# Opening transfers, output tiles, gating of w_out and the static scheduler of a hybrid decoder block

## Chip, cores and metric

The kernel runs on one core of one Trainium2 chip. The metric is the device time of one execution in microseconds (us), the median of the runs. Engines are named as in the profile: PE is TensorE, DVE VectorE, ACT ScalarE, POOL GpSimd, SP SyncE, which issues the transfers.

## The reference

One sequence of 512 tokens, width 1024, passes through a decoder block in float32. A conditioning vector `c` gives six modulation vectors (shift, scale and gate for each of two sub-layers). One projection `w_in` feeds two mixers: sparse attention with an index score and a top-k of 128 keys per query, and a gated linear recurrence. Their outputs are gated and added, go through `w_out`, and a convolutional FFN follows. Cut to that:

```python
c_act = jax.nn.silu(c)
mod = jnp.dot(c_act, w_ada[l]) + b_ada[l]
sh1, sc1, ga1, sh2, sc2, ga2 = [m[:, None, :] for m in jnp.split(mod, 6, axis=-1)]
xn = rms_norm(h, g_mix[l]) * (1.0 + sc1) + sh1
proj = jnp.dot(xn, w_in[l]) + b_in[l]
q, k, v, qi, ki, wi, xr, yr, gate_a, gate_b = jnp.split(proj, cuts, axis=-1)
attn = dsa_attention(q, k, v, qi, ki, wi, rel_bias)      # q_idx, k_idx score; top_k; softmax
xr = causal_dwconv(xr, conv_rnn_w[l], conv_rnn_b[l])
rnn = rg_lru(xr, ...) * jax.nn.gelu(yr)                  # h = scan of a*h + u
merged = (jax.nn.sigmoid(gate_a) * jnp.dot(attn, w_o_attn[l])
          + jax.nn.sigmoid(gate_b) * jnp.dot(rnn, w_o_rnn[l]))
h = h + ga1 * jnp.dot(merged, w_out[l])
xn = rms_norm(h, g_ffn[l]) * (1.0 + sc2) + sh2
up = causal_dwconv(jnp.dot(xn, w_up[l]), conv_ffn_w[l], conv_ffn_b[l])
val, gte = jnp.split(up, 2, axis=-1)
h = h + ga2 * jnp.dot(jax.nn.silu(gte) * val, w_down[l])
return rms_norm(h, g_final)
```

## The kernel before

Every float32 product is three matmuls on TensorE: each operand is split into a rounded high part and a low rest (`xh`, `xl` of the activations, `wh`, `wl` of a weight), and `mm3` adds xh·wh, xl·wh and xh·wl. ScalarE writes the high part of a weight, VectorE subtracts it to get the low part. Weights come as 1 MB transfers of two output tiles each (`wr`; `wo` for w_out; `wa` for pieces of w_ada) into three landing buffers, and their parts lie in six buffers of 128x1024.

Every instruction is first recorded in a `Plan`. Then a list scheduler orders all of them by a rank and by what the cost of each would be, and the kernel is emitted in that order, a fixed order for each engine. An operation may name several engines (`("dve", "pool")`), of which the scheduler chooses one. The rank comes from `P.fix` (the planned time of a matmul) or from `P.soft`, a time that the code writes ahead of a group of operations. Numbers such as `COLD`, `SOON`, `RB`, `IW` and `AW` at the head of the file are such times and widths.

The stages, in TensorE's order:

- Opening. `x` is read in eight halves of 128x512, its row norms are computed, and its tiles `xs` are transposed. `dots` (VectorE) multiplies pieces of w_ada by `crow`, the silu of `c` spread over all partitions, and gives shift and scale (`modc`) for each block `kt` of 128 features. ScalarE makes `xf` from transposed `xs` and `modc`, then `xh`. A first group of seven tiles (`G0`) is multiplied block by block, its block 0 in two halves of 256 tokens.
- The rest of `w_in` in tiles of 128 output features, one `wr` half each: tiles 0 to 19 (`xr`, `yr`, `qi`, `k`, `v`, `q`), then the gates `gb` and `ga` (tiles 20 to 35).
- `rnn_batch` comes twice, each for four blocks: gates `rg` (two products, with `xc` and with `m`), the scan `h`, and `yr*h`. The products of `rg` and `yr` may go to VectorE or GpSimd.
- Index scores, top-k (MAX8 and MATCH_REPLACE8 in turn on VectorE), softmax, and attention run between the tiles.
- Output tiles `wr` (the recurrence) for j = 0 to 7, then `wa` (attention) for j = 0 to 7. `consume` multiplies each by its gate and, for `wa`, adds the two on VectorE or GpSimd and splits the sum into `mh`, `ml`.
- w_out: rows of the weight, `raw`, are multiplied by the gate vector `ga_b`, split into `woh`, `wol`, and used for four row tiles. The result is added to `x` (`xr_`).
- Second norm, FFN up and down projections, final norm.

## Time and profile before

| | |
|---|---|
| median of 3 runs | 808.45 us (807.95 to 808.86) |
| span of the profiled execution, first to last instruction | 807.4 us |
| device time of the profiled execution itself | not shown; its span is 1.05 us under the median |
| PE busy | 778.1 us, 96% |
| DVE busy | 605.1 us, 75% |
| ACT busy | 434.7 us, 54% |
| POOL busy | 83.3 us, 10% |
| bytes moved | 105.23 MB, 130 GB/s on average |

PE is busy in nearly all of the span. The other engines matter where PE waits for them; those waits are few and each can be found in a view of the waits.

### The profile page before, as it was taken

What the parts mean: (1) busy time and instruction counts of PE and PEld (TensorE: products, weight loads), DVE (VectorE), ACT (ScalarE), POOL (GpSimd) and SP (SyncE); (2) the same over time, 40 slices, a digit from 0 to 9 for tenths busy, and PEclk for the clock granted to TensorE, in tenths of its full rate; (3) what the DMA queues carried; (4) which work ended last, traced back from release to release, by engine and by line L of the source; (5) the groups of instructions that cost most, each with busy time, mean ns of one, the idle gap of its engine ahead of it and who ended that gap; (6) DMA issues with size and microseconds to landing.
All of it is one profiled execution on the core that took longest, in us unless ns stands there. A gap on an engine that the chain in (4) does not pass through costs nothing.

```text
span 807.4 us, 9805 instructions
## 1 busy us (share of the span) xinstructions
PE 778.1 (96%) x3576; PEld 646.3 (80%) x3576; DVE 605.1 (75%) x1137; ACT 434.7 (54%) x745; POOL 83.3 (10%) x88
## 2 busy tenths in 40 slices
PE   5999999999799999999899999999999999999996
PEld 3888778888688888888688988888888888888885
DVE  5997975999999989757988777766556688774024
ACT  5679825579499989632427744434444454332013
POOL 2000300034331242003201000000000000000000
PEclk9999989999899999999999999999999999999999
DMA  9973132331121251537174233343222224431002
GB/s 323 391 259 133 53 105 104 105 106 53 52 86 73 106 207 60 203 116 254 73 297 172 102 124 144 153 157 131 104 103 69 89 105 157 146 123 60 12 26 79
DMA packets 21297, 105.23 MB, mean 130 GB/s; under 512 B 2376, under 2 KB 4864, under 8 KB 10624
## 3 DMA queue, kind: packets, MB, share of 16 engines
q1 hardware_dynamic: 21248, 104.60, 36.0%
q8 instruction: 28, 0.46, 0.2%
q14 instruction: 21, 0.17, 0.1%
HBM read 102.47 MB, written 3.69 MB: 131 GB/s over the span
## 4 chain that ended last, share of the span: by engine, by line
PE 77%; DVE 13%; ACT 4%; DMA 3%; issue 2%; POOL 1%; SPq 0%; POOLq 0%; ACTq 0%; DVEq 0%
PE ps L499 76%; DVE h L817 2%; PE ps L511 2%; DVE wl L435 1%; DVE wol L435 1%; DVE wo L435 1%; DVE wa L584 1%; DMA wr<-in_w_up_dram 1%; DMA x<-in_x_dram 1%; DMA wa<-in_wada_dram 1%; DVE rg L435 1%; POOL rstd L570 1%; DVE sc L860 1%; DVE m L859 1%; ACT rg L428 1%
## 5 line engine op out<-in xcount | busy, mean ns | idle before, releaser
L499 PE MATMUL ps<-yl,wh 128*128 128x512 f32 (+1 forms) x376 | 141.8, 377 | 0.3 <-DVE yl L435 0.2
L499 PE MATMUL ps<-yh,wh 128*128 128x512 f32 (+1 forms) x376 | 141.5, 376 | 0.0
L499 PE MATMUL ps<-yh,wl 128*128 128x512 f32 (+1 forms) x376 | 141.3, 376 | 0.0
L435 DVE TENSOR_TENSOR wl<-wr,wh 128x1024 fp32r<-128x1024 f32 (+1 forms) x96 | 117.3, 1222 | 29.2 <-ACT wh L428 29.2
L428 ACT ACTIVATE wh<-wr 128x1024 fp32r<-128x1024 f32 (+1 forms) x96 | 97.8, 1019 | 63.8 <-PE ps L499 60.5
L499 PE MATMUL ps<-xh,wl 128*128 128x512 f32 x288 | 114.7, 398 | 7.9 <-DVE wl L435 7.9
L499 PE MATMUL ps<-xh,wh 128*128 128x512 f32 x288 | 114.8, 399 | 0.0
L499 PE MATMUL ps<-xl,wh 128*128 128x512 f32 x288 | 114.2, 396 | 0.0
L440 DVE SCALAR_TENSOR_TENSOR cv<-ps,ct,cv 128x511 f32<-128x511 f32 (+1 forms) x88 | 65.6, 747 | 42.5 <-ACT cv L428 41.1
L499 PEld LDWEIGHTS ps<-yl,wh 128*128 128x128 f32 x376 | 70.8, 188 | 13.7 <-DVE yl L435 1.0
L499 PEld LDWEIGHTS ps<-yh,wh 128*128 128x128 f32 x376 | 70.8, 188 | 12.9
L499 PEld LDWEIGHTS ps<-yh,wl 128*128 128x128 f32 x376 | 70.8, 188 | 12.7
L499 PEld LDWEIGHTS ps<-xh,wl 128*128 128x128 f32 x288 | 55.4, 192 | 20.6 <-DVE wl L435 8.7
L428 ACT ACTIVATE cv<-ps,ct 128x512 f32<-128x512 f32 x44 | 33.8, 768 | 67.8 <-PE ps L499 67.8
L499 PE MATMUL ps<-dl,acth 128*128 128x512 f32 (+1 forms) x181 | 69.4, 384 | 0.0
L499 PE MATMUL ps<-dh,actl 128*128 128x512 f32 (+1 forms) x181 | 69.4, 383 | 0.0
L499 PE MATMUL ps<-dh,acth 128*128 128x512 f32 (+1 forms) x181 | 69.4, 383 | 0.0
L499 PEld LDWEIGHTS ps<-xl,wh 128*128 128x128 f32 x288 | 55.3, 192 | 10.8
L499 PEld LDWEIGHTS ps<-xh,wh 128*128 128x128 f32 x288 | 55.4, 192 | 10.5
L584 DVE SCALAR_TENSOR_TENSOR wa<-wa,crow 128x1024 f32<-128x1024 f32 x48 | 59.6, 1257 | 2.7 <-DMA wa<-in_wada_dram 2.7
L570 POOL TENSOR_TENSOR rstd<-ms,mhalf 128x1 f32<-128x1 f32 x12 | 9.3, 783 | 415.1 <-DVE ms L440 415.1
L428 ACT ACTIVATE dh<-wd 128x512 fp32r<-128x512 f32 x44 | 25.9, 626 | 35.3 <-PE ps L499 31.5
(242 smaller groups left out, 1440.3 us busy)
## 6 DMA issues: line engine op xcount, KB each, us to landing
wa<-in_wada_dram SPq DMA_DIRECT2D x22, 1024.0 KB, 5.6
wr<-in_w_up_dram SPq DMA_DIRECT2D x22, 1024.0 KB, 4.8
wr<-in_win_dram SPq DMA_DIRECT2D x18, 1024.0 KB, 4.8
wd<-in_w_down_dram SPq DMA_DIRECT2D x11, 1024.0 KB, 4.8
wr<-in_wo_rnn_dram SPq DMA_DIRECT2D x4, 1024.0 KB, 4.8
wo<-in_w_out_dram SPq DMA_DIRECT2D x4, 1024.0 KB, 4.7
x<-in_x_dram SPq DMA_DIRECT2D x8, 256.0 KB, 4.7
wa<-in_wada_dram SPq DMA_DIRECT2D x4, 512.0 KB, 6.4
```

What stands on the lines that cost most here:

```text
L428: nc.scalar.activation(real(dst), real(src), func, **kw)
L435: lambda e: ENG[e].tensor_tensor(real(dst), real(a), real(b), op=op), tag="tt")
L440: lambda e: nc.vector.scalar_tensor_tensor(real(dst), real(a), real(s), real(b), op0=op0, op1=op1), tag="stt")
L499: nc.tensor.matmul(real(ps), real(a), real(b), start=st, stop=sp)
L511: nc.tensor.transpose(real(ps[:, i * 128:(i + 1) * 128]), real(s), real(ident))
L570: lambda: nc.gpsimd.tensor_tensor(real(r), real(ms), real(mhalf), op=ALU.pow), "pool")
L584: vop(1.14, [r, crow], [r, dst], lambda: nc.vector.scalar_tensor_tensor(real(r), real(r), 1.0, real(crow), op0=ALU.mult, op1=ALU.mult, acc ...
L817: vop(0.61, [a, u], [h], lambda h=h, a=a, u=u: nc.vector.tensor_tensor_scan(real(h), real(a), real(u), 0.0, op0=ALU.mult, op1=ALU.add))
L859: vop(0.07 + 0.00104 * W, [a], [m8], lambda m8=m8: nc.vector.max(real(m8), real(a)))
L860: vop(0.07 + 0.00104 * W, [a, m8], [a], lambda m8=m8: nc.vector.match_replace(real(a), real(m8), real(a), TAKEN))
```

## The change

These things change together.

1. Opening transfers: all of `x` for the first two row tiles comes right behind the small table `ct`, then both halves of the first `wa` block, then the rest of `x`, then weights. The relative bias table moves behind the third `wa`. Squares of row tiles 2 and 3 are on ScalarE alone. Eight calls of `transposes` on the identity, 32 instructions, write a bank that is otherwise empty then.
2. Output tiles: `OUTS` gives an order in which `wr` and `wa` tiles alternate in groups. The one of a pair that comes second makes the sum, on VectorE only.
3. The gate of w_out: `ga_b` no longer multiplies the weight; the result of each of the eight output pieces is multiplied by it instead.
4. Scheduler: operations that read two SBUF operands on VectorE or any on GpSimd are marked as sharing a port (`shares_port`), and one is not planned beside the other. The cost of a matmul, a scan, MAX and MATCH_REPLACE is other than before.
5. `INFLATE`, `HORIZON`, `SOON`, `LATER`, `CLOCK` and the step widths of the index and attention stages take other values.
6. Where the scheduler may choose, GpSimd gets one product of the RNN batches instead of twelve.
7. The order of each engine is changed by all of these. On ScalarE 29 table loads stand where 26 stood, one of the new ones ahead of the square roots of the first RNN batch.

```diff
+OUTS = [("wr", (0, 1, 2, 3)), ("wa", (0, 1)), ("wr", (4, 5)), ("wa", (2, 3, 4, 5, 6, 7)), ("wr", (6, 7))]
-COLD = 17.0
+COLD = 8.0
+WARM = 8
+DOT1 = 13.6
+def pass_us(n):
+    return max(0.109, 0.0133 + n / 2400)
...
+    def shares_port(engs, reads, writes, tag):
+
+        wide = [vw(v) for v in reads if isinstance(v, (Buf, View)) and vw(v).bx[1][1] - vw(v).bx[1][0] > 1]
+        sbuf = [v for v in wide if v.buf.kind != "b"]
+        out = set()
+        if "pool" in engs and (sbuf or tag == "pow"):
+            out.add("pool")
+        if "dve" in engs and (len(sbuf) > 1 or (sbuf and tag in ("ts", "sc", "sq", "dot"))):
+            out.add("dve")
+        return out
...
+                if e in o.shares:
+                    f = "pool" if e == "dve" else "dve"
+                    t = max(t, port[f])
+                    for p in avail[f]:
+                        begin = max(free[f], p.ready, p.after)
+                        if f in p.shares and p.rank < o.rank - 2 and not p.allocs and begin < t + 0.3:
+                            t = max(t, begin + p.engs[f])
...
-            P.soft = -59.0 + 2 * t + h + 5 * (t > 1)
+            P.soft = -70.0 + 2 * t + h if t < 2 else -56.0 + 2 * t + h
...
+    xs = [normed(xt[t], LATER, ("act", "dve") if t < 2 else ("act",)) for t in range(TT)]
...
+    for n in range(WARM):
+        P.soft, P.after = -43.0, 3.7
+        transposes(g0ps[-1], [ident] * 4)
+    P.soft, P.after = None, 0.0
...
-            vop(0.61, [a, u], [h], lambda h=h, a=a, u=u: nc.vector.tensor_tensor_scan(
+            vop(1.13, [a, u], [h], lambda h=h, a=a, u=u: nc.vector.tensor_tensor_scan(
...
-        elif kind == "wr":
-            s = got["gb", j]
+        elif kind in ("wr", "wa"):
+            s = got["gb" if kind == "wr" else "ga", j]
             tt(s, ps, s, ALU.mult)
-            mid.append(s)
-        elif kind == "wa":
-            s = got["ga", j]
-            tt(s, ps, s, ALU.mult)
-            tt(s, s, mid[j], ALU.add, ("dve", "pool"))
+            if j not in mid:
+                mid[j] = s
+                return
+            tt(s, s, mid[j], ALU.add)
             hi, lo = t2(F32R, name="mh"), t2(F32R, name="ml")
             split(hi, lo, s)
-            merged.append((hi, lo))
+            merged[j] = (hi, lo)
...
-                tt(r, r, ga_b[0][h], ALU.mult)
                 split(hi, lo, r)
...
-            tt(xr_, ps, xr_, ALU.add)
+            gated = t2(name="gated")
+            tt(gated, ps, ga_b[0][h], ALU.mult)
+            tt(xr_, gated, xr_, ALU.add)
```

How this moves instructions is seen at three places. The first is TensorE's start, before: `csil` matmuls spread the silu of `c`, `oh` is the relative bias, `xs` are row tiles of the normalised `x`, and `w0h` the high part of the first weight.

```order
L499 MATMUL ps_113<-ident_89,csil_98 128x128
L499 MATMUL ps_117<-ident_89,csil_98 128x128
L499 MATMUL ps_113<-ident_89,csil_98 128x128 x3
L499 MATMUL ps_117<-ident_89,csil_98 128x128 x3
L499 MATMUL ps_147<-oh_79,rb_85 128x384
L511 MATMUL ps_163<-ident_89,xs_132 128x128
L511 MATMUL ps_163<-ident_89,xs_155 128x128
L499 MATMUL ps_209<-xh_192,w0h_168 128x256
L499 MATMUL ps_209<-xl_193,w0h_168 128x256
```

The same place in the changed kernel, where `ps_210`, `ps_246` and `ps_251` receive the transposes of block 0.

```order
L530 MATMUL ps_120<-ident_79,csil_98 128x128 x3
L530 MATMUL ps_129<-ident_79,csil_98 128x128 x3
L542 MATMUL ps_110<-ident_79 128x128 x28
L542 MATMUL ps_210<-ident_79,xs_137 128x128
L542 MATMUL ps_210<-ident_79,xs_146 128x128
L542 MATMUL ps_246<-ident_79,xs_235 128x128
L542 MATMUL ps_246<-ident_79,xs_237 128x128
L542 MATMUL ps_251<-ident_79,xs_137 128x128
L542 MATMUL ps_251<-ident_79,xs_146 128x128
L542 MATMUL ps_251<-ident_79,xs_235 128x128
L542 MATMUL ps_251<-ident_79,xs_237 128x128
L530 MATMUL ps_261<-xh_232,w0h_227 128x256
```

Identity transposes now stand ahead of and behind the `csil` matmuls, the relative bias is gone from here, and the eight transposes of all row tiles stand ahead of the first matmul with `xh`, which was behind two of them.

The second place is VectorE in the first RNN batch, before; `wl_1007` is the low part that TensorE waits for at 102.90 us.

```order
L435 TENSOR_TENSOR rg_860<-rg_860,m_938 128x512
L435 TENSOR_TENSOR rg_880<-rg_880,m_953 128x512
L817 SCALAR_TENSOR_TENSOR h_1004<-a_916,rg_846 128x512
L817 SCALAR_TENSOR_TENSOR h_1009<-a_929,rg_860 128x512
L817 SCALAR_TENSOR_TENSOR h_1015<-a_936,rg_872 128x512
L817 SCALAR_TENSOR_TENSOR h_1022<-a_943,rg_880 128x512
L435 TENSOR_TENSOR yr_736<-yr_736,h_1015 128x512
L435 TENSOR_TENSOR yr_776<-yr_776,h_1022 128x512
L440 SCALAR_TENSOR_TENSOR qi_959<-ps_765,ct_81,qi_959 64x512
L440 SCALAR_TENSOR_TENSOR qi_993<-ps_765,ct_81,qi_993 64x512
L440 SCALAR_TENSOR_TENSOR xc_999<-ps_882,ct_81,xc_999 128x511
L435 TENSOR_TENSOR wl_1007<-wr_699,wh_1006 128x1024
```

The same place in the changed kernel, where that low part is `wl_1018`.

```order
L466 TENSOR_TENSOR rg_889<-rg_889,m_967 128x512
L466 TENSOR_TENSOR rg_900<-rg_900,m_975 128x512
L854 SCALAR_TENSOR_TENSOR h_1029<-a_938,rg_867 128x512
L854 SCALAR_TENSOR_TENSOR h_1039<-a_950,rg_877 128x512
L854 SCALAR_TENSOR_TENSOR h_1048<-a_957,rg_889 128x512
L854 SCALAR_TENSOR_TENSOR h_1062<-a_961,rg_900 128x512
L466 TENSOR_TENSOR yr_751<-yr_751,h_1029 128x512
L466 TENSOR_TENSOR yr_757<-yr_757,h_1039 128x512
L466 TENSOR_TENSOR yr_764<-yr_764,h_1048 128x512
L466 TENSOR_TENSOR yr_924<-yr_924,h_1062 128x512
L466 TENSOR_TENSOR wl_1018<-wr_719,wh_1017 128x1024
L471 SCALAR_TENSOR_TENSOR qi_1027<-ps_807,ct_84,qi_1027 64x512
```

All four products of `rg` (two of them above these rows) and all four of `yr` are in VectorE's order, where two and two stood, and the low part of the weight stands directly behind the last of them, ahead of `qi` and `xc`.

The third place is VectorE between the low parts of tiles 22 and 23, before (`sc` is the index score, `m` the eight largest, `q` the queries).

```order
L435 TENSOR_TENSOR wl_1901<-wr_1648,wh_1900 128x1024
L859 MAX m_360_1970<-sc_1531 128x8
L440 SCALAR_TENSOR_TENSOR q_1914<-ps_1773,ct_81,q_1914 64x512
L860 MATCH_REPLACE sc_1531<-m_360_1970,sc_1531 128x384
L440 SCALAR_TENSOR_TENSOR q_1920<-ps_1773,ct_81,q_1920 64x512
L859 MAX m_361_1988<-sc_1531 128x8
L440 SCALAR_TENSOR_TENSOR q_1928<-ps_1824,ct_81,q_1928 64x512
L860 MATCH_REPLACE sc_1531<-m_361_1988,sc_1531 128x384
L435 TENSOR_TENSOR wl_1938<-wr_1648,wh_1937 128x1024
```

In the changed kernel the low parts are `wl_1914` and `wl_1955`. Here stand the last twelve of the rows from the one to the other; behind `wl_1914` come twelve more of the same kinds.

```order
L896 MAX m_361_2063<-sc_1560 128x8
L938 ISA l_2072,nmax_2073<-ps_2041,bm_1990 128x128
L938 ISA nmax_2073 128x1
L897 MATCH_REPLACE sc_1560<-m_361_2063,sc_1560 128x384
L471 SCALAR_TENSOR_TENSOR q_1936<-ps_1804,ct_84,q_1936 64x512
L896 MAX m_362_2087<-sc_1560 128x8
L941 RECIPROCAL sums_2051<-sums_2051 128x1
L897 MATCH_REPLACE sc_1560<-m_362_2087,sc_1560 128x384
L941 RECIPROCAL sums_2070<-sums_2070 128x1
L941 RECIPROCAL sums_2076<-sums_2076 128x1
L941 RECIPROCAL sums_2081<-sums_2081 128x1
L466 TENSOR_TENSOR wl_1955<-wr_1555,wh_1954 128x1024
```

Seven instructions stood between the two; now there are 23, with softmax passes (`ISA`, with `nmax`) and reciprocals among them.

## Rows read from the trace of the kernel before

**Rows 1.** First part of the page: busy us, share of the span, instructions.
```profile
PE 778.1 (96%) x3576; PEld 646.3 (80%) x3576; DVE 605.1 (75%) x1137; ACT 434.7 (54%) x745; POOL 83.3 (10%) x88
```

**Rows 2.** Waits of TensorE: engine, line, waited for; us, times, longest.
```profile
PE ps L499 <- DVE wl L435: 7.9, 2, 4.5
...
PE ps L499 <- DVE wol L435: 2.3, 1, 2.3
```

**Rows 3.** Windows: us, busy of PE, PEld, DVE, ACT, POOL, clock, DMA share, GB/s.
```profile
200.00:220.00 20.00, 15.49 (x62) 12.41 (x61) 19.57 (x41) 7.93 (x17) 7.97 (x9) 0.83 0.15 53
209.00:214.00 5.00, 4.89 (x12) 3.83 (x13) 4.80 (x11) 0.00 (x0) 0.00 (x0) 0.50 0.00 0
```

**Rows 4.** Timeline of TensorE, 99 to 108: start, us, engine, line, instruction, idle before.
```profile
99.13 0.39 PE L499 MATMUL ps<-xl,wh 128*128 128x512 f32 x1
102.90 0.80 PE L499 MATMUL ps<-xh,wl 128*128 128x512 f32 x1 [3.38 <-DVE wl L435]
103.49 0.63 PE L499 MATMUL ps<-xh,wh 128*128 128x512 f32 x1
...
107.76 0.63 PE L499 MATMUL ps<-xl,wh 128*128 128x512 f32 x1
```

**Rows 5.** Timeline of TensorE in the opening.
```profile
15.95 0.58 PE L499 MATMUL ps<-xh,w0h 128*128 128x256 f32 x1 [2.33 <-ACT xh L428]
...
25.03 0.40 PE L499 MATMUL ps<-xh,w0h 128*128 128x512 f32 x1
25.26 0.40 PE L499 MATMUL ps<-xl,w0h 128*128 128x512 f32 x1
```

**Rows 6.** Timeline of VectorE in the first RNN batch; x counts instructions put together.
```profile
88.13 3.49 DVE L435 TENSOR_TENSOR rg<-rg,m 128x512 f32<-128x512 f32 x2
91.55 6.67 DVE L817 TENSOR_TENSOR_SCAN h<-a,rg 128x512 f32<-128x512 f32 x4
98.14 1.26 DVE L435 TENSOR_TENSOR yr<-yr,h 128x512 f32<-128x512 f32 x2
...
101.62 1.22 DVE L435 TENSOR_TENSOR wl<-wr,wh 128x1024 fp32r<-128x1024 f32 x1
```

**Rows 7.** Timeline of GpSimd in the same stretch.
```profile
92.84 4.30 POOL L435 TENSOR_TENSOR yr<-yr,h 128x512 f32<-128x512 f32 x2 [1.76 <-DVE h L817]
```

**Rows 8.** The tile of the scans: ns of one, shortest, median and longest.
```profile
L817 DVE TENSOR_TENSOR_SCAN h<-a,rg x8: 1191/1727/2252, 91.5 to 200.6; 128x512 f32<-128x512 f32 x8
```

**Rows 9.** Timeline of ScalarE in the first RNN batch.
```profile
85.49 1.28 ACT L428 ACT_TABLE_LOAD   x1
```

**Rows 10.** Timeline of VectorE in the second RNN batch.
```profile
174.92 2.10 DVE L435 TENSOR_TENSOR wl<-wr,wh 128x1024 fp32r<-128x1024 f32 x1
...
193.88 2.38 DVE L435 TENSOR_TENSOR rg<-rg,m 128x512 f32<-128x512 f32 x2
196.18 6.66 DVE L817 TENSOR_TENSOR_SCAN h<-a,rg 128x512 f32<-128x512 f32 x4
```

**Rows 11.** VectorE's instructions by line and shape: busy us, mean ns, idle before.
```profile
L435 DVE TENSOR_TENSOR wo<-wo,ga 128x512 f32<-128x512 f32 x16 | 11.6, 750 | 1.7 <-DMA wo<-in_w_out_dram 1.7
...
L859 DVE MAX8 m<-sc 128x8 f32<-128x384 f32 x16 | 8.9, 557 | 0.3
...
L901 DVE CUSTOM_DVE_ANT_0 l<-ps,bm 128x128 f32<-128x128 f32 x8 | 1.8, 281 | 0.0
```

**Rows 12.** GpSimd's instructions by line and shape.
```profile
L435 POOL TENSOR_TENSOR ga<-ga,gb 128x512 f32<-128x512 f32 x8 | 12.8, 1607 | 71.4 <-DVE ga L435 68.9 <-ACT woh L428 2.5
```

**Rows 13.** Last part of the page: transfers, KB each, median us to landing.
```profile
wo<-in_w_out_dram SPq DMA_DIRECT2D x4, 1024.0 KB, 4.7
```

**Rows 14.** Timeline of VectorE in the opening.
```profile
9.88 0.69 DVE L469 SCALAR_TENSOR_TENSOR junk<-x 128x512 f32<-128x512 f32 x1 [1.77 <-DMA x<-in_x_dram]
...
10.70 1.22 DVE L584 SCALAR_TENSOR_TENSOR wa<-wa,crow 128x1024 f32<-128x1024 f32 x1
```

**Rows 15.** Waits of ScalarE.
```profile
ACT wh L428 <- PE ps L499: 60.5, 37, 10.0
```

More of the change, by code (lines that the diff above doesn't have):

```diff
@@ L43 @@
 SHAPES = {"W": [128, 2048], "w": [128, 1024], "t": [128, 512], "b": [128, 512]}
-INFLATE = 1.3
-HORIZON = 32
+INFLATE = 1.19
+HORIZON = 26
 EARLY = 3
 LAST = 5
+OUTS = [("wr", (0, 1, 2, 3)), ("wa", (0, 1)), ("wr", (4, 5)), ("wa", (2, 3, 4, 5, 6, 7)), ("wr", (6, 7))]
 ADA0 = 28
-COLD = 17.0
-SECOND = 0.0
-LATER = 20.93
-CLOCK = 11.0
+COLD = 8.0
+RBIAS = [14.0, 46.0, 48.0]
+WARM = 8
+DOT1 = 13.6
+SECOND = -25.0
+LATER = 19.39
+CLOCK = 12.7
 RB = [3.28, 5.94, 7.96, 11.0, 13.85, 0.61]
-SOON = [17.32, 14.96, 25.0, 9.88]
-ISTEP = {1: 13, 2: 36, 3: 83}
-IW = {1: 18, 2: 46, 3: 37}
+SOON = [20.62, 17.45, 25.0, 11.19]
+ISTEP = {1: 13, 2: 37.5, 3: 88.8}
+IW = {1: 18, 2: 46.8, 3: 42.2}
 ASTEP = {0: 76, 1: 93, 2: 126, 3: 145}
-AW = [8, 16, 15, 29]
-BUMP = [0.2, 0.93]
+AW = [8, 13.5, 18.7, 30.4]
+BUMP = [0.16, 0.81]
 def tile_columns(kind, j):
@@ L154 @@
     __slots__ = ("engs", "emit", "reads", "writes", "deps", "succ", "rank", "idx", "func", "ready", "left",
-                 "fixed", "soft", "hor", "after", "weak", "allocs", "lat", "end", "bufs", "start", "eng", "n", "tag")
+                 "fixed", "soft", "hor", "after", "weak", "allocs", "lat", "end", "bufs", "start", "eng", "n", "tag", "shares")
 LAT = {"pe": {"pe": 0.0, "act": 0.2, "dve": 0.2, "pool": 0.2, "sp": 0.2},
@@ L178, in op @@
         o.n, o.tag = n, tag
+        o.shares = self.shares_port(engs, reads, writes, tag)
         o.soft, o.hor, o.after = self.soft, self.hor, self.after
@@ L244, in order @@
         avail = {e: [] for e in LAT}
+        port = {"dve": 0.0, "pool": 0.0}
         free = {e: 0.0 for e in LAT}
@@ L335, in order @@
             free[e] = o.end
+            if e in o.shares:
+                port[e] = o.end
             for x in o.engs:
@@ L482, in scaled, with vop @@
         P.op({e: c[e] for e in engs}, [src, s], [dst], emit, tag="sc")
-    def vop(cost, reads, writes, fn, eng="dve", n=1):
-        P.op({eng: cost}, reads, writes, lambda e: fn(), n=n, tag="vop")
+    def vop(cost, reads, writes, fn, eng="dve", n=1, tag="vop"):
+        P.op({eng: cost}, reads, writes, lambda e: fn(), n=n, tag=tag)
     def mm(group):
@@ L492, in mm @@
             fp = vw(b).buf.dtype == F32
-            cost += max(0.107, 0.00042 * n) if not fp else max(0.214, 0.00168 * n)
+            cost += 2 * pass_us(2 * n) if fp else pass_us(n)
             reads += [a, b]
@@ L529, in col @@
         return ct[:, o + j:o + j + n]
-    P.soft = -60.0
+    P.soft = -90.0
     dma(ct, cols, 128 * 4 * NCOLS)
@@ L562, in rstd_of @@
         for h, v in enumerate(halves):
-            square(t2(name="junk")[:, :width(v)], v, parts[h])
+            square(t2(name="junk")[:, :width(v)], v, parts[h], engs)
             if h == 0:
@@ L569, in rstd_of, with normed @@
         vop(0.46, [ms, mhalf], [r],
-            lambda: nc.gpsimd.tensor_tensor(real(r), real(ms), real(mhalf), op=ALU.pow), "pool")
+            lambda: nc.gpsimd.tensor_tensor(real(r), real(ms), real(mhalf), op=ALU.pow), "pool", tag="pow")
         return r
-    def normed(halves, after=0.0):
-        r = rstd_of(halves)
+    def normed(halves, after=0.0, engs=("act", "dve")):
+        r = rstd_of(halves, engs)
         o = [t2(name="xs") for _ in range(2)]
@@ L609, in modulate @@
         return hi, lo
-    xs = [normed(xt[t], LATER) for t in range(TT)]
+    xs = [normed(xt[t], LATER, ("act", "dve") if t < 2 else ("act",)) for t in range(TT)]
     rb, oh, bias = cst((128, 128), "rb"), t2(name="oh"), t2(name="bias")
@@ L614, in block_kernel @@
     vop(0.5, [], [oh], lambda: nc.gpsimd.memset(real(oh), 0.0), "pool")
-    P.soft = -54.5
+    P.soft = RBIAS[0]
     dma(rb[:32, :8], rel_bias, 1024)
     dma(oh[:32, :NU], onehot, 32 * 4 * NU)
-    P.soft = -10.0
+    P.soft = RBIAS[1]
     pb = bank()
     mm([(pb[:, :NU], rb, oh[:, :NU], True, True)])
-    P.soft = 16.0
+    P.soft = RBIAS[2]
     act(bias[:8, :NU], pb[:8, :NU], AF.Copy, scale=8.0)
@@ L630, in block_kernel @@
         if kt < 2:
-            P.soft = -55.0 + 15 * kt
+            P.soft = -60.0 + 20.0 * kt
             dma(raw[:, 1, :], wada1[kt, :, 1, :], 1 << 19)
-            P.soft = -54.0 + 15 * kt
+            P.soft = -58.0 + 20.0 * kt
             dma(raw[:, 0, :], wada1[kt, :, 0, :], 1 << 19)
-            P.soft = -52.0 + 15 * kt
+            P.soft = -45.0 + 8 * kt
         else:
@@ L644, in block_kernel @@
         sh, sc = small((128, 1), "sh"), small((128, 1), "sc")
+        P.after = DOT1 if kt else 0.0
         dots(sc, raw, 1)
@@ L648, in block_kernel @@
         tt(modc[:, kt:kt + 1], sh, col("b_ada", kt), ALU.add)
+        P.after = 0.0
         ws = []
@@ L708, in block_kernel @@
     order += [byname["gb", j] for j in range(8)] + [byname["ga", j] for j in range(8)]
-    order += [("wr", j, wo_rnn, j // 2, j % 2, KT) for j in range(8)]
-    order += [("wa", j, wo_attn, j // 2, j % 2, 4) for j in range(8)]
+    for kind, js in OUTS:
+        order += [(kind, j, wo_rnn, j // 2, j % 2, KT) if kind == "wr" else (kind, j, wo_attn, j // 2, j % 2, 4) for j in js]
     raws = {}
@@ L936, in block_kernel @@
     ga_b = [[None, None], [None, None]]
-    mid = []
-    merged = []
+    mid = {}
+    merged = {}
     def consume(kind, j, ps):
@@ L1162, in down @@
         hi, lo = dsplit[f][h]
-        planned(0.00127 * (n.stop - n.start))
+        planned(3 * pass_us(n.stop - n.start))
         mm3(ps[:, n], acts[f][0][:, c], acts[f][1][:, c], hi[:, n], lo[:, n], f == first, f == last)
```

17 lines of the change are left out of this document (9 added, 8 removed).

## The prediction

> **What bounds the kernel now.** The profiled execution has a span of 807.4 us; no device time is shown for that execution itself. The median of the three runs, 808.45 us, lies 1.05 above that span, so I make the sum on the span and add the 1.05 at the end. The page's first part has TensorE busy for 778.1 us of it [rows 1]: some 29 us of idleness, and what a low clock costs behind it, are all that the change can take. I read TensorE's waits next [rows 2]: two waits on the low half of a weight (`wl`) hold 7.9 us, the longer 4.5, and one on `wol` in the w_out stage 2.3. Then the windows [rows 3]: behind the longer one the granted clock is 0.50. The reader is to see that such a wait is paid twice. At the first one [rows 4] TensorE stands for 3.38 us until 102.90; from 103.49 to 107.76 ten matmuls take 4.27, 0.427 each, where in the opening two of the same width start 0.23 apart [rows 5]. About twelve and a half matmuls run at that pace, each 0.20 too slow: 2.5. So **stall 1** costs 5.9. **Stall 2** is the longer wait, 4.5, and the window from 209 to 214 holds 12 matmuls in 4.89 where 21 would fit: 2.2, together 6.7. **Stall 3** is 2.3 and, if it is paid at the rate of stall 1 (2.5 of clock on 3.4 of wait), 1.7 more: 4.0. The opening is the fourth place: from the first matmul of the projection (15.95) to the first of 512 columns (25.03) 9.08 us pass, in which stand 42 matmuls of 256 columns, worth 42 × 0.12 = 5.0 (half of 0.23 each), and some transposes.
>
> VectorE makes `wl`, so I ask what it did before stall 1 [rows 6]. Behind the previous `wl` stand two `rg*m` (3.49), four scans (6.67), two `yr*h` (1.26), `qi` and `xc`, and only at 101.62 the next `wl`. GpSimd runs its own two `yr*h`, 4.30, beside the scans [rows 7]. The shortest scan is 1191 ns, the median 1727 [rows 8]: scans and products are stretched where GpSimd works beside them. Without it a product takes VectorE 0.63 (two in 1.26).
>
> **Part 1, the first RNN batch.** GpSimd loses its `rg*m` and `yr*h`, VectorE gets them, and the next `wl` moves ahead of `qi` and `xc`. From 88.13 the chain is then 4 products (2.5), 4 scans at 1.19 (4.8), 4 products (2.5) and a `wl` (1.22): its end is 99.15. TensorE wants it 0.23 behind the matmul at 99.13, at 99.36. ScalarE gets one more table load ahead of its square roots; one takes 1.28 [rows 9], of which perhaps 0.5 reaches VectorE, since that one still works on a `wl` then: 99.7, a wait of 0.3, for which I charge no slow clock. **Gain 5.6.** Bounds: 5.9, and, if the scans keep 1.73 each with no neighbour, a chain 2.2 longer, so a wait of 2.5 and as much again for the clock: gain 1. I stand near the upper one, since the four scans took 6.67 in all with GpSimd beside only some of them, and the shortest shows what is left alone.
>
> **Part 2, the second batch and the attention stage.** VectorE is 19.57 us busy in the 20 from 200 [rows 3]: it sets the time here. It takes over three `rg*xc`, two `rg*m`, two `yr*h`: 7 × 0.63 = 4.4. It gets back what GpSimd beside it cost [rows 10]: four scans took 6.66 instead of 4.76 (1.9), a `wl` 2.10 instead of 1.22 and a second one nearly so (1.5), two `rg` 2.38 instead of 1.26 (1.1), two `yr` a little: 4.5 to 5, less up to 0.8 for the one `rg*xc` left on GpSimd. One pair of MAX8 and MATCH_REPLACE fewer stands ahead of tile 22 (about 1.1). So the `wl` that TensorE waited for is ready about 1.2 earlier. But behind it, between that `wl` and the next, the changed order puts 23 instructions of top-k, softmax and `q` where seven stood. With the durations by shape (MAX8 0.56, MATCH_REPLACE8 as much, a softmax pass 0.28) [rows 11] that stretch is about 10 us instead of 5.7, and the next one 9.4 instead of 4.9. Some of this only comes earlier, and TensorE has attention matmuls of its own in there: counted against those, VectorE is 4.2 further behind at tile 24 than at tile 22. So the 4.5 of wait shrinks at tile 22 and comes back at 23 and 24, with a slow clock behind it. **Gain 0.5**; bounds: a loss of 4.2 (no relief from GpSimd's leaving), and 6.7 (the stall is gone).
>
> **Part 3, w_out.** Sixteen `wo*ga` on VectorE go (11.6 us) [rows 11], eight `ga` sums go from GpSimd (12.8) [rows 12] to VectorE, eight `gated` products come in behind the matmuls, all of 128x512. Ahead of the wait on `wol`, VectorE loses about six of the sixteen and some 3 us of stretching, and takes five or six sums: some 3 us better, which ends the 2.3. What is late next is the weight itself: the buffers of 1 MB are three, shared by `wr`, `wa` and `wo`, and with the output tiles alternating the last `wr` is split later; a `wo` issued on its release has 4.7 us to landing [rows 13] and a split on two engines behind that. I count 2.5 to 4 with the clock against the 4 of now. **Gain 0.7**, bounds −2 and 4. `gated` adds one product of 0.63 ahead of the second norm; TensorE has the matmuls of the other row tiles there, and the view of its waits names none on the second norm's products, so I cost it at nothing, and at 0.7 if that cover is gone.
>
> **Part 4, the opening.** The first dot began at 10.70, beside the square of `x`'s last half of row tile 1, begun at 9.88 [rows 14]. Now that half is asked for ahead of `wa`, so it is there a little sooner, about 9; but `crow`, from which the dots come, stands on ScalarE behind its square and a scaling that needs its norm. With a square, a power on GpSimd and a scaling at about 0.6 each plus hand-overs, and two copies for `crow`, I get 12.2; two dots of 1.2 make 14.6; `xf`, `w0h`, `xh` at 0.5 to 0.6 make 16.3; and TensorE's order puts the transposes of all four row tiles, the last from an `xs` that ScalarE makes behind `xh`, ahead of the first matmul: about 17.4, 1.4 later than 15.95. Behind it 42 matmuls stand in a row. At the high clock they end at 22.4, 2.6 before 25.03; with four microseconds at the low clock, as after stall 1, at 24.5. The warm-up of 32 transposes begins about 3.3 and is through near 10 to 13, whatever the clock, and then TensorE stands for microseconds, as it did before the low clock of stall 1. So I take the low clock: **gain 0.5**, bounds −1 (another 1.5 us on ScalarE) and 2.6.
>
> A rule of the Trainium skill bears on this: its page "TensorE: Matmul & The Clock Gate", Part 4 (PE-mode transpose), says that transposes don't count as work for the clock gate. No run here shows transposes alone for long; by the rule the warm-up would do nothing for the clock and the sum has 0.5 here, without it up to 2.6.
>
> **Sum.** 807.4 − 5.6 − 0.5 − 0.7 − 0.5 = 800.1, and 1.05 around it: **801.1 us**. FFN and tail keep their instructions.
>
> **The rivals.** *All stalls go.* If GpSimd's leaving relieves VectorE by more than I count, stalls 2 and 3 end too: 5.6 + 6.7 + 4 + 0.5 = 16.8 gives 791.7, one of them alone 795 to 798. For it: every stretched row of VectorE has GpSimd beside it. Against it: the longer queue between tiles 22 and 24.
> *Slower: the gain is handed back at tile 24.* VectorE sets the time from some 140 us on. If it does not move up by the 5.6 of part 1, TensorE only arrives earlier and waits 5.6 longer, and if the relief is nothing too, 4.2 more: 808.45 + 4.2 − 1.2 = 811.5. It decides once the relief is under about 3 of the 5 us and VectorE stays where it was. Against it: ScalarE, which writes the high half ahead of each `wl`, waits 60.5 us for TensorE [rows 15], so VectorE's work there should come earlier with TensorE.
> *No change.* Scans stay long by themselves (gain 1) and the rest cancels: 807 to 810.
>
> **Chances.** Forecast, stall 1 gone and the others about as they are: 0.48, 797 to 804.5. More stalls gone: 0.24, 790.5 to 797. Half of stall 1: 0.10, 804.5 to 806.8. No change within 0.2% (1.6 us, about what a measurement of this kernel can tell): 0.07. Slower: 0.11. The range, 791 to 808.5, leaves out the slower case and the fast one's edge. Faster 0.82, same 0.07, slower 0.11.
>
> **What would show it.** TensorE's wait near 100 us gone or under 1, and scans of 1.2 us with no GpSimd beside them; a wait on `wl` in the ten to twenty microseconds behind the old stall 2; in w_out a wait through `woh` for a landing; the first projection matmul near 17.4 and the low clock behind it. Scans that stay long alone would make part 1 wrong, tiles 22 to 24 without a wait part 2, an early high clock part 4.

## The result and the profile after

The changed kernel takes 796.81 us (median of four runs, 796.1 to 797.54) against 808.54 (807.95 to 808.86): a ratio of 0.9851, 95% interval 0.9839 to 0.9863, or 11.7 us. The profiled execution has a span of 794.3 us, 13.1 less than before; it was itself timed at 796.1. In every run here that has both numbers the time of an execution lies 1.7 to 2.2 us above its span, mostly 1.8, so the profiled execution before, with a span of 807.4, took about 809.2 by estimate, 0.7 above its kernel's median, and the one after lies 0.7 under its own. That is why the spans show 13.1 and the medians 11.7.

First part of the page of the changed kernel, which answers to [rows 1]:

```profile
PE 775.3 (98%) x3608; PEld 645.3 (81%) x3608; DVE 595.8 (75%) x1144; ACT 439.2 (55%) x752; POOL 48.3 (6%) x69
```

GpSimd's work went from 83.3 to 48.3 us. VectorE took over some of it and is still busy for less time. TensorE's waits, which answer to [rows 2]:

```profile
PE ps L542 <- DVE xs L511: 5.2, 1, 5.2
PE ps L542 <- ACT l L459: 1.6, 5, 0.5
...
PE ps L530 <- DVE wl L466: 1.1, 1, 1.1
PE ps L530 <- DVE q L471: 0.9, 1, 0.9
```

The 7.9 us on `wl` are 1.1, and `wol` is gone from the list. The largest wait now lies in the opening, where TensorE has run out of transposes. Windows of the changed kernel, with the granted clock as the third figure from the end:

```profile
15.00:17.00 2.00, 1.12 (x4) 0.83 (x5) 1.43 (x4) 1.85 (x5) 0.23 (x1) 0.50 1.02 396
17.00:20.00 3.00, 3.00 (x17) 3.00 (x16) 2.98 (x7) 1.90 (x4) 0.00 (x0) 0.52 1.06 419
...
200.00:220.00 20.00, 18.01 (x83) 13.99 (x81) 19.76 (x62) 17.03 (x42) 1.88 (x3) 1.00 0.15 53
...
380.00:400.00 20.00, 20.00 (x90) 16.53 (x90) 17.61 (x35) 4.93 (x8) 0.00 (x0) 1.00 0.90 332
```

Behind the opening the clock is at its upper level in all these windows: 200 to 220 had 0.83 in [rows 3]. VectorE in the first RNN batch of the changed kernel, against [rows 6]:

```profile
87.46 2.50 DVE L466 TENSOR_TENSOR rg<-rg,m 128x512 f32<-128x512 f32 x4 [0.60 <-ACT m L459]
89.88 4.57 DVE L854 TENSOR_TENSOR_SCAN h<-a,rg 128x512 f32<-128x512 f32 x4
94.36 2.48 DVE L466 TENSOR_TENSOR yr<-yr,h 128x512 f32<-128x512 f32 x4
96.75 1.22 DVE L466 TENSOR_TENSOR wl<-wr,wh 128x1024 fp32r<-128x1024 f32 x1
```

Four products, four scans, four products and the weight end at 97.97. Four scans take 4.57 where they took 6.67. TensorE in the opening of the changed kernel, against [rows 5]:

```profile
15.21 0.48 PE L542 MATMUL ps<-ident,xs 128*128 128x128 f32 x1 [5.19 <-DVE xs L511]
...
17.34 0.56 PE L530 MATMUL ps<-xh,w0h 128*128 128x256 f32 x1
...
23.94 0.47 PE L530 MATMUL ps<-xh,w0h 128*128 128x512 f32 x1
```

To see where the 13.1 us came from, TensorE's own landmarks serve: the first matmul of 512 columns, the first of w_out (`woh`), the first of the FFN (`yh`). All of TensorE's work on output tiles lies ahead of the second in both kernels. The tiles `woh` and `yh` before (ns shortest, median, longest; first and last start in us):

```profile
L499 PE MATMUL ps<-woh,mh x64: 387/389/632, 387.1 to 436.7; 128*128 128x512 f32 x64
...
L499 PE MATMUL ps<-yh,wh x376: 278/389/478, 437.5 to 680.2; 128*128 128x512 f32 x164, 128*128 128x256 f32 x24
```

The same two tiles after:

```profile
L530 PE MATMUL ps<-woh,mh x64: 389/389/476, 378.7 to 423.2; 128*128 128x512 f32 x64
...
L530 PE MATMUL ps<-yh,wh x376: 276/389/476, 424.0 to 667.2; 128*128 128x512 f32 x164, 128*128 128x256 f32 x24
```

| stretch | before | after | gain | predicted |
|---|---|---|---|---|
| start to first matmul of 512 columns | 25.03 | 23.94 | 1.1 | 0.5 |
| from there to the first w_out matmul | 362.1 | 354.8 | 7.3 | 6.1 |
| w_out to the first FFN matmul | 50.4 | 45.3 | 5.1 | 0.7 |
| FFN to the end of the span | 369.9 | 370.3 | −0.4 | 0 |

In the second row stall 1 is 5.9, which is gone whole, and 1.4 remain for the second batch and attention, predicted 0.5. Stall 2, costed at 6.7, is gone as well, so some 5.3 of the two came back elsewhere in that stretch.

### The profile page after: what moved, and what is told of

Its sections match the earlier page's. It is cut to its first block, busy times and chain, and to the rows that moved or that the text cites. A ratio compares the mean times of both kernels' runs of the same rounds, so it can differ in the third digit from the quotient of the medians.

```text
span 794.3 us, 9871 instructions
## 1 busy us (share of the span) xinstructions
PE 775.3 (98%) x3608; PEld 645.3 (81%) x3608; DVE 595.8 (75%) x1144; ACT 439.2 (55%) x752; POOL 48.3 (6%) x69
## 4 chain that ended last, share of the span: by engine, by line
PE 79%; DVE 11%; ACT 5%; issue 2%; DMA 1%; SPq 0%; POOLq 0%; POOL 0%; DVEq 0%; ACTq 0%
PE ps L530 78%; DVE sc L897 2%; DVE wl L466 2%; PE ps L542 2%; DVE m L896 1%; ACT l L459 1%; DVE sc L471 1%; DMA x<-in_x_dram 1%; ACT L459 1%; DVE h L854 1%; DVE q L471 1%; DVE rg L466 1%; ACT wh L459 1%; ACT gb L459 0%; DVE al L466 0%
## 5 line engine op out<-in xcount | busy, mean ns | idle before, releaser
L466 DVE TENSOR_TENSOR wl<-wr,wh 128x1024 fp32r<-128x1024 f32 (+1 forms) x96 | 113.1, 1179 | 21.6 <-ACT wh L459 21.5
L530 PE MATMUL ps<-xh,wl 128*128 128x512 f32 x288 | 112.4, 390 | 1.1 <-DVE wl L466 1.1
L530 PE MATMUL ps<-xl,wh 128*128 128x512 f32 x288 | 112.3, 390 | 0.0
L471 DVE SCALAR_TENSOR_TENSOR cv<-ps,ct,cv 128x511 f32<-128x511 f32 x88 | 65.8, 748 | 48.3 <-ACT cv L459 47.1
L615 DVE SCALAR_TENSOR_TENSOR wa<-wa,crow 128x1024 f32<-128x1024 f32 x48 | 57.8, 1221 | 4.9 <-DMA wa<-in_wada_dram 2.4
L466 DVE TENSOR_TENSOR dl<-wd,dh 128x512 fp32r<-128x512 f32 x44 | 29.0, 688 | 15.9 <-PE ps L530 14.1
```

Source lines behind the costliest of these rows:

```text
L466: lambda e: ENG[e].tensor_tensor(real(dst), real(a), real(b), op=op), tag="tt")
L471: lambda e: nc.vector.scalar_tensor_tensor(real(dst), real(a), real(s), real(b), op0=op0, op1=op1), tag="stt")
L530: nc.tensor.matmul(real(ps), real(a), real(b), start=st, stop=sp)
L615: vop(1.14, [r, crow], [r, dst], lambda: nc.vector.scalar_tensor_tensor(real(r), real(r), 1.0, real(crow), op0=ALU.mult, op1=ALU.mult, acc ...
```

## The experiments

All are timed against the kernel before on the same chip; the changed kernel was timed in its own session, so a run is set against it by ratios, by medians that come from two sessions, or by stretches of the two traces. The three theories at stake are: GpSimd's instructions beside VectorE's are what cost the time (mine, for the RNN batches); the gate's sixteen products cause the w_out wait; and, for the opening, transposes do or do not keep the clock.

**Opening without the warm-up** (`e1_no_warm`).

```diff
-WARM = 8
+WARM = 0
```

> The changed kernel without the 32 transposes of the identity; the rest as in it. Theory A: the warm-up is worth nothing, since TensorE stands still for 5.2 us behind it and the clock is low again when the first projection matmul starts at 17.3; expected 796.8 within 0.5 us, first matmul at 17.3, low clock behind it. Theory B: the low stretch behind that matmul is shorter with the warm-up (it ended at 19.8, 2.5 us after the first matmul, where it was 4.1 in the kernel before); without it some seven more matmuls of 256 columns run 0.09 too slow, 0.7 us or a little more, 797.5 to 798.

Measured: 796.48 us (796.18 to 796.5), ratio 0.9853 (0.9831 to 0.9876). The first projection matmul came at 17.15, the low clock lasted until about 20.5, and the first matmul of 512 columns stood at 24.10, 0.16 later than with the warm-up. The span was 794.7 against 794.3. Theory A: nothing that the time can tell. Theory B is right in direction only: the low stretch is 0.8 us longer, but the matmuls began 0.2 earlier.

**A longer warm-up** (`e2_long_warm`).

```diff
+WARM2 = 12
...
+    for n in range(WARM2):
+        P.soft, P.after = -38.0, 9.9
+        transposes(g0ps[-1], [ident] * 4)
```

> The changed kernel with 48 more transposes of the identity, asked for between the first and the second transposes of x, so that TensorE has work until about 14.7. Theory A: any work of TensorE holds the clock; then the first matmuls of 256 columns stand 0.12 apart from the start instead of 0.21, and the 12 slow ones save 1.1 us: 795.5 to 796. Theory B: transposes do not count as work for the clock; the matmuls start at the low clock as now, and the time is the same or, if the first transposes of x come late behind the warm-up, some tenths longer: 796.8 to 797.5.

Measured: 801.12 us (798.85 to 803.07), ratio 0.9920 (0.9890 to 0.9949). Two of TensorE's waits in this run:

```profile
PE ps L531 <- DVE wl L467: 3.7, 1, 3.7
PE ps L531 <- DVE xl L467: 1.7, 1, 1.7
```

The clock did what theory A says, since the first matmuls behind the wait stood 0.12 apart. But the planner, which counts the transposes, moved other instructions: `xl` came late by 1.7, the first matmul of 512 columns stood at 24.25, and a wait of 3.7 on `wl` grew in the second batch. The time lies above what either theory said. The run tells the clock but not the price, so a cleaner one follows below.

**RNN products on VectorE, nothing else** (`e3_before_rnn_on_dve`, in the kernel before; the same edit for `rg*m` and `yr*h`).

```diff
-            tt(u, u, xc, ALU.mult, ("dve", "pool"))
+            tt(u, u, xc, ALU.mult)
```

> The kernel before with one edit: the products of rg and yr in the RNN batches may go to VectorE only. Theory A: the scans were stretched by GpSimd's products beside them; they now take 1.13 to 1.2 us each, the wait on wl near 100 us shrinks from 3.4 to 1 or 2 (wl still stands behind qi and xc) and its slow clock with it: a gain of 3 to 5 us there, and 0 to 2 in the second batch, 802 to 806 in all. Theory B: the scans stay at 1.7 whoever works beside them; VectorE has four products more, the wait grows to 5 or 6: 811 to 814.

Measured: 802.88 us, ratio 0.9935 (0.9911 to 0.9958). The scans of this run, against [rows 8]:

```profile
L817 DVE TENSOR_TENSOR_SCAN h<-a,rg x8: 1193/1201/1691, 90.5 to 192.9; 128x512 f32<-128x512 f32 x8
```

The median scan fell from 1727 to 1201 ns. Its waits on `wl` and `wol`:

```profile
PE ps L499 <- DVE wl L435: 5.7, 2, 4.2
PE ps L499 <- DVE wol L435: 3.7, 3, 2.1
```

Of the two waits on `wl` the longer, 4.2, is still that of the second batch; the first has become 1.5, so that stall 1, 5.9 with its slow clock, shrank to that. VectorE begins the weight's low part at 99.64 where it was 101.62, still behind `qi` and `xc`. Theory A, with its numbers. The waits on `wol` have grown from 2.3 to 3.7, and w_out's stretch from 50.4 to 51.6.

**Half of the RNN products on GpSimd in the changed kernel** (`e4_after_rnn_half_on_pool`).

```diff
-            tt(u, u, m, ALU.mult, ("dve", "pool"))
+            tt(u, u, m, ALU.mult, ("pool",) if j % 2 else ("dve",))
...
-            tt(y, y, h, ALU.mult, ("dve", "pool"))
+            tt(y, y, h, ALU.mult, ("pool",) if j % 2 == 0 else ("dve",))
```

> The changed kernel with half of the products rg*m and of yr*h of both RNN batches on GpSimd, as in the kernel before. Theory A: GpSimd's products beside the scans cost VectorE more than they take off it; the wait on the low half of a weight near 95 to 100 us comes back with 2 to 4 us and its slow clock, the second batch loses 1 to 3: 801 to 805. Theory B: what ended that wait is only that the weight's low half stands ahead of qi and xc; then the time grows by 2 us at most, 797 to 799.

Measured: 806.18 us, ratio 0.9977 (0.9962 to 0.9992); 9 us of the gain are gone, more than either theory said. Its waits on `wl`, and its scans:

```profile
PE ps L530 <- DVE wl L466: 4.6, 2, 4.0
```

```profile
L854 DVE TENSOR_TENSOR_SCAN h<-a,rg x8: 1193/1218/2256, 91.3 to 206.2; 128x512 f32<-128x512 f32 x8
```

The wait of 4.0 us is on a `wl` that VectorE began at 102.22. Of the first three scans ahead of it, 4.50 together, two took 1.2 and the third, beside GpSimd's first `yr*h`, 2.26; the fourth came late, behind `qi` and `xc`, and the weight behind it. So two things delay that weight, some 2.4 us of stretching (1.1 in the scans, 1.3 in two `rg*m`, 2.56 together) and the place that the scheduler gave to the fourth scan, and the run doesn't separate what each costs TensorE.

**The port rule off** (`e12_after_no_port_rule`).

```diff
-        o.shares = self.shares_port(engs, reads, writes, tag)
+        o.shares = set()
```

> The changed kernel with the port rule of the scheduler switched off (no operation is marked as sharing a port); costs, numbers, opening, gate and tile order as in it. GpSimd then gets seventeen products of the RNN batches and of rg instead of one, fifteen of them beside VectorE's scans or products. Theory A: that is the part of the scheduler that counts; scans are stretched again, the waits on wl near 100 and 200 come back: 804 to 809. Theory B: the numbers tuned with it leave room; 798 to 801.

Measured: 800.41 us, ratio 0.9894 (0.9878 to 0.9911). Wait and scans of this run:

```profile
PE ps L530 <- DVE wl L466: 5.8, 2, 5.2
```

```profile
L854 DVE TENSOR_TENSOR_SCAN h<-a,rg x8: 1192/2248/2322, 87.8 to 193.5; 128x512 f32<-128x512 f32 x8
```

Here VectorE's scans and fifteen products of GpSimd (seventeen were expected) lie side by side and the scan's median is 2248 ns. The wait on `wl` in the second batch is 5.2; the one of the first batch is only 0.6, since the weight stands ahead of `qi` and `xc` here too. That is 3.6 us of the gain. The time is theory B's; of theory A the stretched scans and the wait near 200 came true, and the wait near 100 hardly. The port rule matters in the second batch.

**The gate moved, nothing else** (`e5_before_gate_moved`, in the kernel before).

```diff
-                tt(r, r, ga_b[0][h], ALU.mult)
                 split(hi, lo, r)
...
-            tt(xr_, ps, xr_, ALU.add)
+            gated = t2(name="gated")
+            tt(gated, ps, ga_b[0][h], ALU.mult)
+            tt(xr_, gated, xr_, ALU.add)
```

> The kernel before with one edit: the gate multiplies w_out's outputs (eight products) and no longer the weight (sixteen). Theory A: VectorE's load ahead of the first w_out tiles was the whole cause of the wait on wol; the wait of 2.3 us and its slow clock go, 804 to 805. Theory B (the prediction's): a wait for the landing or the split of w_out takes its place; gain 0 to 1, 807.5 to 808.5.

Measured: 810.23 us, ratio 1.0022 (1.0012 to 1.0031). Sixteen products fewer on VectorE, and nothing gained; the time is even 0.2% longer, above both ranges:

```profile
PE ps L499 <- DVE wol L435: 2.6, 3, 1.3
```

One wait of 2.3 became three of 0.6 to 1.3. They are on `wol` and not on a landing, so theory A is refuted, and theory B is right that something took the wait's place and wrong in what it was. From the first w_out matmul to the first of the FFN it takes 50.9, where it took 50.4.

**The gate back on the weight in the changed kernel** (`e6_after_gate_on_weight`, the reverse edit).

> The changed kernel with the gate back on w_out's weight, all else as in it. Theory A: the sixteen products on VectorE are what made the wait in w_out; it comes back with 2 to 4 us and a slow clock: 799.5 to 802. Theory B: alternating output tiles and sums on VectorE alone give enough room; at most 1 us longer, 797 to 797.8.

Measured: 797.03 us, ratio 0.9857 (0.9843 to 0.9872), the same as the changed kernel. No wait on `wol` or `woh` appeared among TensorE's waits. Theory B: the gate's place is worth a few tenths, 0.7 us in w_out's stretch (46.0 against 45.3).

**Output tiles in sequence** (`e7_after_outputs_in_sequence`).

```diff
-OUTS = [("wr", (0, 1, 2, 3)), ("wa", (0, 1)), ("wr", (4, 5)), ("wa", (2, 3, 4, 5, 6, 7)), ("wr", (6, 7))]
+OUTS = [("wr", (0, 1, 2, 3, 4, 5, 6, 7)), ("wa", (0, 1, 2, 3, 4, 5, 6, 7))]
```

> The changed kernel with all wr output tiles ahead of all wa tiles, as in the kernel before. Theory A: the alternation spreads VectorE's work and frees landing buffers earlier for w_out; without it TensorE waits at the start of w_out for 1 to 3 us: 798 to 801. Theory B: the moved gate alone is enough; 796.8 within 0.6 us.

Measured: 798.9 us, ratio 0.9871 (0.9854 to 0.9887). The first line below is from TensorE's waits, the second the granted clock (third figure from the end) in a window of the opening:

```profile
PE ps L530 <- DVE wol L466: 0.6, 2, 0.4
...
20.00:22.40 2.40, 2.40 (x13) 2.40 (x12) 1.90 (x7) 2.07 (x4) 0.00 (x0) 0.51 0.99 356
```

Two waits on `wol`, 0.6 us together, came back, and w_out's stretch takes 46.5 where it takes 45.3. The medians differ by 2 us, at theory A's lower end, but the intervals of the two ratios overlap, and 1.1 of what the profiled execution is longer arises in the opening, which has the same instructions in the same order in both kernels: here the low clock lasted until 22.4 and not until 19.9. So the tile order is worth about 1.2 in w_out, and the 1.1 has nothing to do with it.

**The sums on GpSimd** (`e8_after_sums_on_pool`).

```diff
-            tt(s, s, mid[j], ALU.add)
+            tt(s, s, mid[j], ALU.add, ("pool",))
```

> The changed kernel with the eight sums of the output tiles on GpSimd only. Theory A: GpSimd's sums (1.6 us each before) stretch VectorE's products beside them, and the chain from a tile to its split gets 1 us longer; a wait in w_out of 1 to 3 us: 798 to 800. Theory B: VectorE has room now; 796.8 within 0.6 us.

Measured: 802.99 us, ratio 0.9926 (0.9911 to 0.9941). Eight sums on another engine cost 6 us, more than theory A said. TensorE's waits in w_out:

```profile
PE ps L530 <- DVE wol L466: 2.3, 1, 2.3
...
PE ps L530 <- ACT woh L459: 1.4, 1, 1.4
```

How this goes is seen on three engines. One sum on GpSimd:

```profile
376.63 4.68 POOL L466 TENSOR_TENSOR gb<-gb,ga 128x512 f32<-128x512 f32 x1 [7.92 <-DVE gb L466]
```

VectorE beside it:

```profile
376.47 3.69 DVE L466 TENSOR_TENSOR wol<-wo,woh 128x512 fp32r<-128x512 f32 x6
382.01 0.69 DVE L466 TENSOR_TENSOR ml<-gb,mh 128x512 fp32r<-128x512 f32 x1 [1.85 <-ACT mh L459]
...
383.82 2.95 DVE L466 TENSOR_TENSOR wol<-wo,woh 128x512 fp32r<-128x512 f32 x3
```

And ScalarE, which waits for the sum:

```profile
381.34 0.63 ACT L459 ACTIVATE mh<-gb 128x512 fp32r<-128x512 f32 x1 [3.04 <-POOL gb L466]
381.88 1.13 ACT L459 ACTIVATE woh<-wo 128x512 fp32r<-128x512 f32 x2
```

VectorE's six subtractions run at 0.6 each, undisturbed, and the sum, 1.6 in the rows of its like [rows 12], takes 4.68: it gets through when they are done. `mh` waits 3.04 for it on ScalarE (in the changed kernel the same `mh` starts at 376.63), the next two `woh` stand behind `mh`, VectorE then has nothing to subtract for 1.85, and TensorE waits for both. Three microseconds later it is the other way round: three subtractions beside the next sum take 2.95. Either engine loses, by turns, and both lie on w_out's chain. From the first w_out matmul to the first of the FFN it takes 51.2 here, against 45.3.

**The sums on VectorE, nothing else** (`e9_before_sums_on_dve`, in the kernel before).

```diff
-            tt(s, s, mid[j], ALU.add, ("dve", "pool"))
+            tt(s, s, mid[j], ALU.add)
```

> The kernel before with one edit: the eight sums of the output tiles on VectorE only. The run with GpSimd's sums in the changed kernel cost 6 us, and the moved gate alone gained nothing. Theory A: those sums on GpSimd are the cause of the w_out wait also before; the waits of 2.3 and 0.3 and their slow clock go, 804 to 805.5. Theory B: with sixteen gate products still on VectorE it cannot take eight sums more; a wait on wol of 2 us or more stays, 807 to 809.

Measured: 805.74 us, ratio 0.9962 (0.9947 to 0.9977).

```profile
PE ps L499 <- DVE wol L435: 0.3, 1, 0.3
```

With all sixteen gate products still on VectorE, and eight sums added, the wait of 2.3 is 0.3. Theory A, 3.4 us by the medians (its range missed by 0.2); w_out's stretch takes 46.1 where it took 50.4.

**Three edits together** (`e10_before_three_edits`: the edits of `e3`, `e5` and `e9` in the kernel before).

> The kernel before with three edits together: RNN products on VectorE only, sums of the output tiles on VectorE only, the gate on w_out's outputs. Scheduler, its numbers, opening and tile order stay as before. Theory A: GpSimd beside VectorE is what most of the change removed; gain of 5.8 (RNN alone, as measured) plus 4 in w_out: 798 to 800. Theory B: the scheduler's new costs and the alternating tiles are needed for w_out; gain 5 to 7, 801.5 to 804.

Measured: 799.2 us, ratio 0.9880 (0.9865 to 0.9894): 9.9 of the 11.7 us, with the old scheduler, opening and tile order: theory A. No wait on `wol` is left, and w_out's stretch takes 45.3 as in the changed kernel. What remains is the second batch:

```profile
PE ps L499 <- DVE wl L435: 5.5, 2, 4.0
```

**The clock held through the opening** (`e11_after_clock_held`). The transposes stand in TensorE's order alone; no other instruction moved on any engine.

```diff
+    def fill(ps, n, follow):
+        def emit(e):
+            for i in range(n):
+                nc.tensor.transpose(real(ps[:, i % 4 * 128:i % 4 * 128 + 128]), real(ident), real(ident))
+        return P.op({"pe": 0.0}, [ident], [ps], emit, n=n, tag="tr", follow=follow)
...
+            if kt == 0 and a == 0:
+                last_tr[0] = fill(g0ps[-1], 48, last_tr[0])
```

> The changed kernel with 48 transposes of the identity more on TensorE, between the first two and the next transposes of x, and no other instruction moved on any engine. They fill the 5.2 us in which TensorE stands. Theory A: the clock is still high at 17.3; the twelve slow matmuls and five transposes gain 1.2 to 1.6 us before the first matmul of 512 columns and, since TensorE hardly idles until 198, in the span too, less what VectorE's queue takes back by then: 795.2 to 796.3. Theory B: the gain of the opening is lost at the wait of 1.15 on wl near 200: 796.8 within 0.4.

Measured: 795.92 us (795.3 to 795.97), ratio 0.9838 (0.9823 to 0.9852). TensorE in its opening:

```profile
11.47 5.40 PE L549 MATMUL ps<-ident 128*128 128x128 f32 x48
16.71 0.82 PE L542 MATMUL ps<-ident,xs 128*128 128x128 f32 x6
17.28 0.36 PE L530 MATMUL ps<-xh,w0h 128*128 128x256 f32 x1
17.48 0.29 PE L530 MATMUL ps<-xl,w0h 128*128 128x256 f32 x1
...
22.75 0.47 PE L530 MATMUL ps<-xh,w0h 128*128 128x512 f32 x1
```

The granted clock of three of its windows:

```profile
10.00:15.00 5.00, 5.00 (x48) 5.00 (x47) 3.42 (x11) 3.67 (x11) 0.91 (x2) 1.00 1.05 402
...
17.00:20.00 3.00, 3.00 (x28) 3.00 (x27) 2.68 (x6) 1.95 (x4) 0.00 (x0) 1.00 1.06 415
...
200.00:220.00 20.00, 19.02 (x85) 15.55 (x86) 19.76 (x63) 17.02 (x43) 2.94 (x3) 0.91 0.15 54
```

The projection starts at 17.28, as in the changed kernel, but at the upper level, and the 512-column matmuls start 1.19 earlier (22.75 against 23.94). In the spans of the profiled executions only 0.2 of that is left (794.1 against 794.3), in the medians 0.9, with runs that do not overlap. So theory A in the opening. In the profiled execution 1.0 of it is lost again ahead of w_out, whose first matmul comes at 378.5 against 378.7: behind the wait on `wl` near 200 the clock falls here (0.91 in the window above), and in the changed kernel's profile it stays at 1.00. That is what theory B said; how often it happens isn't settled, since the profiled execution of the changed kernel is the fastest of its four. By its median it is the fastest version here; the intervals of its ratio and the changed kernel's overlap.

## Why the prediction was right, and where it was mis-sized

The time lies in the range and the sign is right; the gain on the spans is 13.1 where the sum had 7.3 (11.7 by the medians), and one term makes most of the difference. But the picture that I gave the best chance, stall 1 gone and the others about as they are, is not what came: all three stalls are gone, as in the rival of that name, and 796.81 lies 0.2 inside that rival's band. It did not reach the rival's 791.7 because some 5 us came back as small losses between the batches and w_out. The 1.05 added at the end of the sum mixed two executions; from span to time of one execution it is 1.8.

- **Part 1, 5.6 predicted, 5.9.** The chain was to end at 99.15 to 99.7 and ended at 97.97: it began 0.67 earlier, at 87.46, and was 0.5 shorter, with scans 1.14 apart. No wait was left. The scans are short for the reason given: `e3` shows them at 1201 ns with GpSimd's products gone, `e12` at 2248 with them back. For the wait itself the weight's new place counts as much (in `e3` it comes 2.0 earlier, and `qi` and `xc` ahead of it still hold it for 2.2), and each of the two alone does most of it: products off GpSimd, weight still behind `qi` and `xc`, leaves 1.5 (`e3`); weight ahead of them, products on GpSimd, leaves 0.6 (`e12`).
- **Part 2, 0.5 predicted, 1.4: near in size, by another way.** The predicted return of the wait on `wl` at tiles 23 and 24 did not come. What the changed kernel has there are small waits, 0.93 on `q`, 1.15 on `wl` at 201.45, and five on the softmax's `l`, none with a slow clock behind it. So stall 2 went with its 6.7, and about 5.3 came back: TensorE's idle time in the stretch outside the two old waits grew by 3.0, from 1.3 to 4.3, and the rest is running time, most of it slower steps in the softmax's transposes (9.4 us for 80 of them, where they took 7.9). My count of 4.2 us by which VectorE would fall behind was too high; which part of it was wrong no run separates, and the 0.5 itself follows from none of the numbers ahead of it. `e10`, which has the old scheduler, still waits 4.0 in that batch, and `e12`, without the port rule, 5.2, so the scheduler's change is what ended that wait. Its costs and the numbers that changed with it were not tried apart.
- **Part 3, 0.7 predicted, 5.1: the term that failed.** I wrote that VectorE, some 3 us better off, would end the wait on `wol`, and that the weight's landing would be late next and cost 2.5 to 4 of the 4.0. The wait ended; the second half was wrong. The landing is in time for TensorE: three of w_out's four transfers are issued from 363.45 on, 8 to 15 us ahead of the first w_out matmul at 378.7, as SyncE's timeline after shows. ScalarE waits for the fourth, TensorE for none.

```profile
363.45 0.33 SPq L445 DMA_DIRECT2D wo<-in_w_out_dram  x1
...
367.75 2.62 SPq L445 DMA_DIRECT2D wo<-in_w_out_dram  x2
...
380.56 0.33 SPq L445 DMA_DIRECT2D wo<-in_w_out_dram  x1
...
385.32 2.19 ACT L459 ACTIVATE woh<-wo 128x512 fp32r<-128x512 f32 x4 [3.56 <-DMA wo<-in_w_out_dram]
```

  And the number of VectorE's products was not the cause: taking the sixteen gate products off VectorE gained nothing alone (`e5`) and putting them back cost a few tenths (`e6`). The eight sums on GpSimd were: alone, moved to VectorE, they give 3.4 (`e9`), and moved back they cost 6.2 (`e8`). I had priced them as 3 us of stretching on VectorE. In the kernel before, the stretching stands right ahead of the wait: a `wol` took 1.75 beside a sum, where its like take 0.68, and TensorE waited for it.

```profile
389.46 1.64 POOL L435 TENSOR_TENSOR ga<-ga,gb 128x512 f32<-128x512 f32 x1 [2.43 <-DVE ga L435]
...
389.90 1.75 DVE L435 TENSOR_TENSOR wol<-wo,woh 128x512 fp32r<-128x512 f32 x1
...
391.70 0.80 PE L499 MATMUL ps<-wol,mh 128*128 128x512 f32 x1 [2.30 <-DVE wol L435]
```

  `e8` shows a second way that I left out: the sum itself, its `mh` and everything queued behind `mh` on ScalarE come late. The upper bound that I gave this term, 4, was too low, since it held only that one wait and its clock: the stretch from w_out's first matmul to the FFN's lasted 50.4 and takes 45.3. `e9` alone gets 4.3 of these 5.1.
- **Part 4, 0.5 predicted, 1.1.** The first projection matmul was predicted at 17.4 and came at 17.34, at the low clock, as said. The low stretch was shorter than the four microseconds that I took: it ended at 19.9. That is partly luck. `e6` and `e7` have the same order of instructions in the opening; in their profiled executions the low clock ended at 19.8 and 22.4, and the first matmul of 512 columns stood at 23.93 and 25.03, in `e7` no earlier than before. What of the new opening moved the start from 15.95 to 17.34 was not tried, beyond the warm-up.
- **The rule of the Trainium skill** ("TensorE: Matmul & The Clock Gate", Part 4) that transposes don't count as work for the clock: the runs here disagree. In `e11` nothing but transposes runs from 11.47 to 16.71, the granted clock is 1.00 and the matmuls behind stand 0.12 apart from the second on; without them (the changed kernel) it is 0.50 to 0.52 between 15 and 20. The measurement decides. The bound of 2.6 us that I put on this part is nearly reached once the clock is held: from 25.03 before to 22.75 in `e11` is 2.3.
- **The norm behind w_out** was costed at nothing for `gated`, 0.7 without cover. The changed kernel's TensorE has no wait on that norm's products in the list of its waits, so the cover held. From the FFN's start to the end it lost 0.4; `e6`, which has no `gated`, takes 370.4 there and the changed kernel 370.3, so that loss is not that product's. Its cause stays open.
